# Attention's first loads and the projection's weights, issued during the stage before

## The chip, the cores and the metric

One program on one core of a Trainium2 chip. The time is the device time of one launch in microseconds (us); the median of three runs is compared. The engines have a queue each and run it in order: TensorE (PE, matrix products), VectorE (DVE), ScalarE (ACT), GpSimd (POOL) and SyncE (SP, which only issues transfers). A transfer (DMA) is issued by one of these engines and moves data between DRAM and the on-chip memory SBUF; those that POOL issues share one queue (q0, software_dynamic, in the profile), those of SP another (q1, hardware_dynamic). TensorE adds its products up in PSUM banks.

## The reference

One decoder layer over 2048 tokens of width 1024 in float32. The part that the change touches is the first of three sub-layers: one input projection, forgetting attention (8 heads of 64) beside a gated linear attention (4 heads), and one output projection.

```python
def forgetting_attention(q, k, v, f_logit):
    ...
    c = jnp.cumsum(log_f, axis=-1)
    ...
        s = jnp.einsum('bhqd,bhkd->bhqk', q[:, :, q0:q1], k[:, :, :q1], preferred_element_type=jnp.float32) * scale
        s = s + c[:, :, q0:q1, None] - c[:, :, None, :q1]
        ...
        p = jax.nn.softmax(jnp.where(causal, s, -jnp.inf), axis=-1)
        outs.append(jnp.einsum('bhqk,bhkd->bhqd', p.astype(v.dtype), v[:, :, :q1]))
    ...
def hybrid_mixer(...):
    fq, fk, fv, ff, gq, gk, gv, gg, ga = jnp.split(h @ w_in, offsets, axis=-1)
    fox = rms_norm(forgetting_attention(...), fox_out_gain)
    gla = rms_norm(gla_chunked(...), gla_out_gain) * jax.nn.silu(gg)
    return jnp.concatenate([fox, gla], axis=-1) @ w_out
```

Then follow cross-attention into 256 memory tokens (`w_xk`, `w_xv`, ...) and a mixture of 16 experts, whose routing needs small constant tables (index ramps, masks, ones).

## The kernel before

float32 operands are split into a high part (rounded to float32r) and a low part (the rest), and a product is three matmuls: high by high, low by high, high by low (`mm3`, L90 to L92). `split` makes the high part on ACT (L68, L71) and the low part on DVE (L69, L72).

**Stage 1** (to about 711 us) makes the projections. The columns of FoX's keys come last: 16 tiles of two heads by 512 tokens, token chunk by token chunk. Each is split into `o1` buffers and stored by SP (L170) to the DRAM scratch tensors `kh_d` and `kl_d`, [8 heads, rows, 2048]; the queries went to `qh_d` and `ql_d` before, the values to `fv_d`. The linear attention runs beside it on all engines; POOL's last operation for it is at L439.

**Stage 2** is the forgetting attention. Its 16 units are a head pair `p` (4) by a query chunk `c` of 512 (4). `load` (L492) fetches a unit's queries `q1`, `q2` and keys `k1`, `k2` of 256 to 272 KB each, unit 0's on POOL, the others on SP; the values `v` always on POOL, a quarter for each chunk of the first head pair, 1 MB at once for a later pair. Loads run two units ahead (AHEAD = 2). For each unit, `maxima` makes the scores a first time (`ps_a`, L526 and L527) and reduces them on DVE (L529, L531) to the rows' maxima; TensorE turns these round (`pmt`, L537), ACT and DVE split them (`mh`, `ml`), and POOL's queue writes them as two rows of 4 KB into `q2` (L541). `probs` then makes the scores again with the maxima subtracted inside the product (`ps_b`, L570 without and L571 with these two rows), takes the exponential on ACT (`pT`, L573), masks and sums on POOL and DVE, and multiplies by the values (`po`, L557). The unit's result `fe_o` is scaled (L612 to L621) and stored to `yT_d` by SP (L622). A scheduler hangs steps of the later units' maxima (`side`) between the steps of a unit's `probs`, so each engine's order is set when the program is built. `memory_in` prepares the 256 memory tokens in the last four units.

`route_init` (L1045 to L1079) makes the routing tables with some 9 small operations on POOL and as many on DVE. It is called last in stage 2, but depends on nothing in it, and the tables' memory is that of stage 1's last inputs, so that the scheduler has put it at the stage's start, ahead of POOL's first loads.

**Stage 3a** multiplies the joined outputs by `w_out`. Its eight row blocks are loaded by SP into the two buffers `wst` (L690) and split into `woh` and `wol`; a block's load waits for the split two before it. `enter` loads a tile of 128 tokens (`yT`, `y`, `x`; tile 0 on POOL, the rest on SP), and `mixed` makes two halves of 24 matmuls each into `ps`, adds them to `x` (L743) and stores `x` from POOL (L745). The memory tokens' keys and values (`ps_m`, L811, weights `mw` loaded by SP at L799 into two buffers) run beside it.

Of the kernel before, what the change touches and what calls it, by code (L numbers as in the profile page):

```python
# [25 lines left out]
def f32(ap):  # L26
    return ap.bitcast(F32)
# [26 lines left out]
class Trunk:  # L54
# [74 lines left out]
    def stage1(self):  # L129
# [3 lines left out]
        with tc.tile_pool(name="xT", bufs=1) as xp, tc.tile_pool(name="w1", bufs=2) as wp, \  # L133
# [25 lines left out]
            def ttype(ws, m, c, dst, parts=None, scale=1.0):  # L159

                ps = pp.tile([128, 512], F32, name="ps_mm", bufs=3)
                for k in range(KT):
                    self.mm3(ps, ws[k][:, 0, m * 128:(m + 1) * 128], ws[k][:, 1, m * 128:(m + 1) * 128],
                             xh[c][:, k], xl[c][:, k], k == 0, k == KT - 1)
                if parts:
                    hi, lo = (op[0].tile([128, 512], F32R, tag="o1", name="o1", bufs=3) for _ in range(2))
                    self.split(hi, lo, ps, scale)
                    for h in range(2):
                        for t, o in zip(parts, (hi, lo)):
                            nc.sync.dma_start(t[dst + h, 0:64, c * 512:(c + 1) * 512], f32(o)[h * 64:h * 64 + 64])  # L170
                    return
                o = op[0].tile([128, 512], F32, name="o1", bufs=n_o[0])
                evac(o, ps)
                nc.sync.dma_start(dst, o)
# [14 lines left out]
            with tc.tile_pool(name="o1a", bufs=2) as op[0], tc.tile_pool(name="xin", bufs=2) as ip, tc.tile_pool(name="psx1", bufs=2, space=PSUM) as px:  # L189
# [29 lines left out]
                def narrow(c):  # L219
                    cs = slice(c * 512, (c + 1) * 512)  # L220
                    ps = pp.tile([48, 512], F32, name="ps_mm", bufs=3)
                    for k in range(KT):
                        self.mm3(ps, wnh[:, k], wnl[:, k], xh[c][:, k], xl[c][:, k], k == 0, k == KT - 1)
                    o = op[0].tile([48, 512], F32, tag="o1", name="o1", bufs=n_o[0])
                    evac(o, ps)

                    t8, m8 = ip.tile([8, 512], F32, name="t8", bufs=1), ip.tile([8, 512], F32, name="m8", bufs=1)
                    c8 = ip.tile([8, 512], F32, name="c8", bufs=2)
                    nc.scalar.activation(t8, o[0:8], AF.Abs, bias=bf)
                    nc.vector.tensor_scalar(m8, o[0:8], bf, 0.0, op0=OP.add, op1=OP.min)  # L230
                    nc.scalar.activation(t8, t8, AF.Exp, scale=-1.0)
                    nc.scalar.activation(t8, t8, AF.Ln, bias=1.0)
                    nc.vector.tensor_tensor(m8, m8, t8, OP.subtract)
                    nc.vector.tensor_tensor_scan(c8, one8, m8, self.c_last[:, 511:512] if c else 0.0, OP.mult, OP.add)
                    self.c_last = c8
                    ch, cl = (ip.tile([8, 512], F32R, tag=tag, name=nm, bufs=1) for tag, nm in (("t8", "ch"), ("m8", "cl")))
                    self.split(ch, cl, c8, -1.0)
                    for r, t in ((64, ch), (65, cl)):
                        nc.sync.dma_start(self.kl_d[:, r, cs], f32(t))
                    nc.sync.dma_start(self.ga_d[:, cs], o[32:48])  # L240

                pin = self.tc.keep_in_program_order
# [6 lines left out]
                for c in range(4):  # L249
                    cs = slice(c * 512, (c + 1) * 512)  # L250
                    tn = turn(c + 1) if c < 3 else iter(())
                    for m in range(2):
                        for n in range(2):
# [3 lines left out]
                            if (c, m, n) == (0, 0, 0):  # L257
# [12 lines left out]

                                for t, r in ((self.qh_d, 64), (self.qh_d, 65), (self.kl_d, 66), (self.kl_d, 67)):
                                    for b in range(4):
                                        nc.gpsimd.dma_start(t[:, r, b * 512:(b + 1) * 512], one8)
                                w3 = w_in.rearrange("(t p) n -> p t n", p=128)
                                pin(nc.sync.dma_start(wn[:, :, 0:8], w3[:, :, FF:FF + 8]))
                                pin(nc.sync.dma_start(wn[:, :, 32:48], w3[:, :, GA:GA + 16]))
# [197 lines left out]
    def stage2(self):  # L474
# [3 lines left out]
        with tc.tile_pool(name="fx", bufs=1, reuse_waits="tile") as fp, \  # L478
# [13 lines left out]
            def load(u):  # L492

                p, c = u["p"], u["c"]
                cs = slice(c * 512, (c + 1) * 512)
                issue = nc.sync.dma_start if p or c else nc.gpsimd.dma_start
                dma = lambda out, src: issue(f32(out), src.rearrange("h d s -> d h s"))
                hs = slice(2 * p, 2 * p + 2)
                k1, k2 = K[p, c] = [big[f"{nm}{c}{p % 2 if c < 3 else 0}"]() for nm in ("k1", "k2")]
                q1, q2 = u["q"] = [big[f"{nm}{c}"]() for nm in ("q1", "q2")]  # L500
                dma(q1[0:64], self.qh_d[hs, 0:64, cs])
                dma(q1[64:128], self.ql_d[hs, :, cs])
                for d in (0, 64):
                    dma(k1[d:d + 64], self.kh_d[hs, :, cs])
                dma(q2[0:66], self.qh_d[hs, :, cs])
                dma(k2[0:68], self.kl_d[hs, :, cs])
                if c == 0:
                    V[p] = big[f"v{p % 2}"]()
                if c == 0 or p == 0:
# [33 lines left out]
            def probs(u):  # L543
# [73 lines left out]
                nc.gpsimd.tensor_tensor(w, r, r, OP.mult)  # L617
                yield
                nc.vector.scalar_tensor_tensor(w, w, -0.5, l2, op0=OP.mult, op1=OP.mult)
                nc.gpsimd.tensor_tensor(o, o, r, OP.mult)  # L620
                nc.vector.scalar_tensor_tensor(o, w, 1.5, o, op0=OP.add, op1=OP.mult)  # L621
                nc.sync.dma_start(self.yT_d[p * 128:p * 128 + 128, c * 512:(c + 1) * 512], o)  # L622

            ms = [fp.tile([128, 128], F32, name=f"m{i}", bufs=1) for i in range(2)]
            for m in ms:
                nc.gpsimd.memset(m, 0.0)
# [10 lines left out]
            mem = self.memory_in(fp, pp)  # L637
            def ahead():

                for u in units[:AHEAD]:  # L640
                    load(u)
                for n, u in enumerate(units):
                    if n + AHEAD < len(units):
                        load(units[n + AHEAD])
                    yield from maxima(u)
                    u["ready"] = True

            side, tail, due = ahead(), iter(()), 2.0
            for n, u in enumerate(units):

# [16 lines left out]
                pass  # L667
            for _ in mem:
                pass
            self.route_init(self.rp)  # L670


    def load_w(self, pool, hi, lo, src, gain, width, tag="wst"):
# [8 lines left out]
    def stage3a(self):  # L682
        tc, a = self.tc, self.a
        with tc.tile_pool(name="wo", bufs=1, reuse_waits="tile") as wp, tc.tile_pool(name="p3a", bufs=2, reuse_waits="tile") as ip, \
                tc.tile_pool(name="ps3a", bufs=2, space=PSUM, reuse_waits="tile") as pp:
            mem = self.memory_out(pp)
            wh, wl = [], []
            for k in range(KT):
                st = wp.tile([128, D], F32, name="wst", bufs=2)
                self.loaded = self.nc.sync.dma_start(st, a["w_out"].rearrange("l k n -> (l k) n")[k * 128:(k + 1) * 128])  # L690
                for ws, nm in ((wh, "h"), (wl, "l")):
                    ws.append(wp.tile([128, D], F32R, name=f"wo{nm}{k}"))
                self.split(wh[k], wl[k], st, self.gcol("fox_out_gain", k) if k < 4 else self.gcol("gla_out_gain", k - 4))
                if k % 4 == 3:
                    next(mem)
# [99 lines left out]
    def memory_weights(self, n):  # L795

        w = self.memory_block().rearrange("p (t n) -> p t n", t=KT)
        hs = slice(n % 4 * 128, n % 4 * 128 + 128)
        self.nc.sync.dma_start(w, self.a[("w_xk", "w_xv")[n // 4]].rearrange("l (t p) n -> p (l t) n", p=128)[:, :, hs])  # L799
        return w  # L800

    def memory_out(self, pp):
# [790 lines left out]
    def run(self, stages=("1", "2", "m", "3a", "3b", "4")):  # L1593
        with self.tc.tile_pool(name="const", bufs=1) as self.cpool, \
# [1 line left out]


            for nm, rows in (("qh_d", 66), ("ql_d", 64), ("kh_d", 64), ("kl_d", 68)):
                setattr(self, nm, self.dpool.tile([8, rows, S], F32, name=nm))
            self.consts()  # L1600
            for nm, shape in (("fv_d", [S, 512]), ("gqk_d", [2, 2, 128, S]), ("gv_d", [S, 512]),
                              ("gg_d", [S, 512]), ("ga_d", [16, S]), ("y_d", [S, 512]), ("yT_d", [512, S]), ("h1_d", [S, D]), ("h2_d", [S, D])):
# [43 lines left out]
```

## Time and profile before

| | us |
|---|---|
| median of three runs | 2461.46 (2458.09 to 2462.5) |
| the profiled execution | 2460.61 |
| its span on the profile | 2458.8 |
| TensorE busy in the span | 2325.2 (95%) |
| DVE, ACT, POOL busy | 1431.4 (58%), 955.4 (39%), 655.9 (27%) |
| mean granted TensorE clock | 0.973 of full |

TensorE works for 95% of the span, so what is left are the places in which it stands still or runs at a lower granted clock. The profile's list of 40 slices shows where: two slices in which TensorE is busy for less than 6 tenths, one between stages 1 and 2 (from about 711 us) and one between stages 2 and 3a (from about 1204 us). A granted clock of 1.00 is 2.4 GHz, 0.50 is 1.2 GHz; a stretch between the two holds some of both. "Waits" name the instruction that an engine stood before and the one that released it; a landing time is from a transfer's issue to its arrival.

### The profile page before, as it was taken

Reading aid. Unit: us, or ns where it says so; the run is one execution under the profiler, and the core shown is the slowest. Engines: PE = TensorE matmul, PEld = TensorE weight load, DVE = VectorE, ACT = ScalarE, POOL = GpSimd, SP = SyncE. Lnnn points to the kernel's source line nnn. Section 1 sums busy time; section 2 is a strip of 40 time slices with the busy share of each in tenths; the row PEclk is TensorE's granted clock in tenths of the full one; section 3 lists DMA queues with packets and bytes.
Section 4 is the critical chain, followed back from the end, with each engine's and each line's share of the span. In section 5 each row is a group of like instructions: output and inputs, shape, how many; then the busy total and the mean of one; then the engine's idle time right before and its main releaser. Section 6 shows DMA issues by size and latency. Waiting matters only on the chain. (4 is left out here: it accounts for less than half of the span.)

```text
span 2458.8 us, 39269 instructions
## 1 busy us (share of the span) xinstructions
PE 2325.2 (95%) x14569; PEld 1875.8 (76%) x14569; DVE 1431.4 (58%) x3561; ACT 955.4 (39%) x2058; POOL 655.9 (27%) x758
## 2 busy tenths in 40 slices
PE   7999999999978999999799999999599999999997
PEld 5778887777756656565478888888499989889996
DVE  5430035656526878778442236556567868768775
ACT  5321023434312444444431135544354545444543
POOL 2000012122213566676500000111322233324132
PEclk9999999999987999999999999999799999999998
DMA  5222122445465132311174521111478888879784
GB/s 180 72 93 69 69 83 83 135 114 133 103 161 131 49 92 59 82 35 53 62 241 126 146 109 53 52 53 53 141 238 260 247 271 257 247 250 270 259 237 133
DMA packets 287626, 337.81 MB, mean 137 GB/s; under 512 B 33264, under 2 KB 208938, under 8 KB 287429
## 3 DMA queue, kind: packets, MB, share of 16 engines
q1 hardware_dynamic: 258485, 257.26, 35.2%
q0 software_dynamic: 28944, 77.98, 10.8%
q8 instruction: 116, 1.90, 0.3%
q14 instruction: 81, 0.66, 0.1%
HBM read 252.27 MB, written 93.02 MB: 140 GB/s over the span
## 5 line engine op out<-in xcount | busy, mean ns | idle before, releaser
L90 PE MATMUL gu<-xTh,wer 128*128 128x288 f32 x1024 | 303.3, 301 | 0.5 <-ACT xTh L68 0.5
L91 PE MATMUL gu<-xTl,wer 128*128 128x288 f32 x1024 | 302.8, 297 | 0.0
L92 PE MATMUL gu<-xTh,wer 128*128 128x288 f32 x1024 | 301.9, 296 | 0.0
L69 DVE TENSOR_TENSOR wer<-wes,wer 128x1024 fp32r<-128x1024 f32 x192 | 232.1, 1220 | 37.4 <-ACT wer L68 37.2
L68 ACT ACTIVATE wer<-wes 128x1024 fp32r<-128x1024 f32 x192 | 198.0, 1052 | 112.2 <-PE yd L92 48.1
L573 ACT ACTIVATE pT<-ps_b 128x512 f32<-128x512 f32 (+3 forms) x320 | 159.7, 532 | 172.5 <-PE ps_b L571 169.1
L90 PEld LDWEIGHTS gu<-xTh,wer 128*128 128x128 f32 x1024 | 192.0, 189 | 3.8 <-ACT xTh L68 0.9
L91 PEld LDWEIGHTS gu<-xTl,wer 128*128 128x128 f32 x1024 | 192.9, 188 | 2.0 <-DVE xTl L69 0.6
L92 PEld LDWEIGHTS gu<-xTh,wer 128*128 128x128 f32 x1024 | 192.9, 188 | 1.8
L592 POOL TENSOR_TENSOR l<-l,pT 128x512 f32<-128x512 f32 (+3 forms) x128 | 151.7, 1185 | 55.1 <-ACT pT L573 48.7
L529 DVE TENSOR_REDUCE mm<-ps_a 128x1 f32<-128x512 f32 x192 | 128.0, 682 | 44.5 <-PE ps_a L527 43.5
L90 PE MATMUL ps_mm<-xh,w1r 128*128 128x512 f32 x384 | 153.3, 402 | 0.5 <-ACT xh L68 0.5
L91 PE MATMUL ps_mm<-xl,w1r 128*128 128x512 f32 x384 | 153.1, 399 | 0.0
L92 PE MATMUL ps_mm<-xh,w1r 128*128 128x512 f32 x384 | 152.4, 399 | 0.0
L91 PE MATMUL ps_mm<-w1r,xh 128*128 128x512 f32 x384 | 150.1, 393 | 0.0
L92 PE MATMUL ps_mm<-w1r,xl 128*128 128x512 f32 x384 | 149.8, 392 | 0.0
L90 PE MATMUL ps_mm<-w1r,xh 128*128 128x512 f32 x384 | 148.3, 392 | 0.0
L526 PE MATMUL ps_a<-k,q 128*128 128x512 f32 (+2 forms) x320 | 129.4, 407 | 16.2 <-DMA k<-kh_d 12.2
L557 PE MATMUL po<-pT,v 128*64 128x512 f32 (+3 forms) x640 | 132.2, 556 | 5.7 <-POOL pT L576 5.4
L527 PE MATMUL ps_a<-k,q 66*128 66x512 f32 (+2 forms) x320 | 124.8, 394 | 13.4 <-DMA k<-kl_d 13.4
L570 PE MATMUL ps_b<-q,k 128*128 128x512 f32 (+3 forms) x320 | 126.3, 403 | 4.0 <-ACT pT L573 4.0
L592 DVE TENSOR_TENSOR l<-l,pT 128x512 f32<-128x512 f32 (+3 forms) x128 | 109.0, 852 | 21.1 <-ACT pT L573 12.5
(429 smaller groups left out, 5599.7 us busy)
## 6 DMA issues: line engine op xcount, KB each, us to landing
wes<-in_w_expert_down_dram SPq DMA_DIRECT2D x64, 512.0 KB
wes<-in_w_expert_gate_dram SPq DMA_DIRECT2D x62, 512.0 KB
wes<-in_w_expert_up_dram SPq DMA_DIRECT2D x62, 512.0 KB
yr_d<-ye SPq DMA_DIRECT2D x32, 512.0 KB
w1s<-in_w_in_dram SPq DMA_DIRECT2D x48, 256.0 KB
xt<-in_x_dram SPq DMA_DIRECT2D x16, 512.0 KB
h_d<-x POOLq DMA_DIRECT2D x16, 512.0 KB, 3.5
h<-h_d SPq DMA_DIRECT2D x16, 512.0 KB
```

Of the source, the lines that this page charges most:

```text
L68: nc.scalar.activation(hi, src, AF.Copy)
L69: nc.vector.tensor_tensor(lo, src, f32(hi), OP.subtract)
L90: mm(ps, ah, bh, start=start, stop=False)
L91: mm(ps, ah, bl, start=False, stop=False)
L92: mm(ps, al, bh, start=False, stop=stop)
L526: nc.tensor.matmul(ps[:, :w], q1[:, i, qs], k1[:, i, :w], start=True, stop=False)
L527: nc.tensor.matmul(ps[:, :w], q2[0:66, i, qs], k2[0:66, i, :w], start=False, stop=True)
L529: nc.vector.tensor_reduce(mm[:, i, b, j:j + 1], ps[:, :w], AX.X, OP.max)
L557: ins = nc.tensor.matmul(po[i * 64:i * 64 + 64, off:], V[p][:, kb, i * 64:i * 64 + 64], pts[i][:, off:], start=new and o == 0, stop=len(to ...
L570: nc.tensor.matmul(ps[:, off:], k1[:, i, ks], q1[:, i, off:], start=True, stop=False)
L573: nc.scalar.activation(pt[:, off:], ps[:, off:], AF.Exp)
L592: add(sums[i][:, off:], sums[i][:, off:], pt[:, off:], OP.add)
```

## The change

Four things are altered.

1. The scratch tensors `qh_d`, `ql_d`, `kh_d`, `kl_d` become four tensors each, one for a chunk of 512 tokens, so that a load of chunk 0 depends on the stores of chunk 0 alone.
2. The loads of units 0 to 2 are written ahead of everything else in stage 2 and go to POOL (unit 3 and all later ones to SP); `route_init` is held until the last unit's last two operations are issued.
3. `yT_d` is stored from ACT instead of SP.
4. `w_out` is loaded into four buffers, two of them the `x3` tiles of the token loop; the split weights of blocks 4 to 7 lie in a pool of their own. From the third on, the memory weights `mw` are loaded by POOL instead of SP.

```diff
-                            nc.sync.dma_start(t[dst + h, 0:64, c * 512:(c + 1) * 512], f32(o)[h * 64:h * 64 + 64])
+                            nc.sync.dma_start(t[c][dst + h, 0:64], f32(o)[h * 64:h * 64 + 64])
...
-                cs = slice(c * 512, (c + 1) * 512)
-                issue = nc.sync.dma_start if p or c else nc.gpsimd.dma_start
+                issue = nc.sync.dma_start if p or c == 3 else nc.gpsimd.dma_start
...
-                dma(q1[0:64], self.qh_d[hs, 0:64, cs])
+                dma(q1[0:64], self.qh_d[c][hs, 0:64])
...
-                nc.gpsimd.tensor_tensor(o, o, r, OP.mult)
-                nc.vector.scalar_tensor_tensor(o, w, 1.5, o, op0=OP.add, op1=OP.mult)
-                nc.sync.dma_start(self.yT_d[p * 128:p * 128 + 128, c * 512:(c + 1) * 512], o)
-
+                last[:] = nc.gpsimd.tensor_tensor(o, o, r, OP.mult), nc.vector.scalar_tensor_tensor(o, w, 1.5, o, op0=OP.add, op1=OP.mult)
+                nc.scalar.dma_start(self.yT_d[p * 128:p * 128 + 128, c * 512:(c + 1) * 512], o)
+
+            for u in units[:AHEAD + 1]:
+                load(u)
...
-                for u in units[:AHEAD]:
-                    load(u)
                 for n, u in enumerate(units):
-                    if n + AHEAD < len(units):
+                    if n and n + AHEAD < len(units):
...
-            self.route_init(self.rp)
+
+            with tc.issue_after(last[0].ins), tc.issue_after(last[1].ins):
+                self.route_init(self.rp)
...
-                st = wp.tile([128, D], F32, name="wst", bufs=2)
+                st = (wp if k % 4 < 2 else ip).tile([128, D], F32, tag=("wst", "x3")[k % 4 // 2], name="wst", bufs=2)
...
-                    ws.append(wp.tile([128, D], F32R, name=f"wo{nm}{k}"))
+                    ws.append((wp, wp2)[k // 4].tile([128, D], F32R, name=f"wo{nm}{k}"))
...
-        self.nc.sync.dma_start(w, self.a[("w_xk", "w_xv")[n // 4]].rearrange("l (t p) n -> p (l t) n", p=128)[:, :, hs])
+        (self.nc.sync if n < 2 else self.nc.gpsimd).dma_start(w, self.a[("w_xk", "w_xv")[n // 4]].rearrange("l (t p) n -> p (l t) n", p=128)[:, :, hs])
...
-                setattr(self, nm, self.dpool.tile([8, rows, S], F32, name=nm))
+                setattr(self, nm, [self.dpool.tile([8, rows, 512], F32, name=f"{nm}{c}") for c in range(4)])
```

POOL's queue at the start of stage 2, before (the two rows at the top are stage 2's constants; routing tables stand ahead of them; `x4` are the four quarters of the first pair's values, and the 16-block `v` is the second pair's 1 MB):

```order
134 L633 MEMSET ones_6661 128x64
135 L634 MEMSET mean_6662 128x128
136 L497 DMA q_6672<-qh_d 64x2x512
137 L497 DMA q_6672<-ql_d 64x2x512
138 L497 DMA k_6670<-kh_d 64x2x512 x2
139 L497 DMA q_6673<-qh_d 66x2x512
140 L497 DMA k_6671<-kl_d 68x2x512
141 L512 DMA v_6680<-fv_d 128x4x128 x4
142 L512 DMA v_6910<-fv_d 128x16x128
143 L636 MEMSET mean_6662 64x64 x2
144 L541 DMA q_6673<-mh 1x8x128
145 L541 DMA q_6673<-ml 1x8x128
```

After, the same queue from the last of unit 2's loads on; the loads of units 0, 1 and 2, six of them and a quarter of `v` for each unit, stand ahead of this piece, right behind stage 1's last operation at L439:

```order
151 L496 DMA k_6692<-kl_d_74 68x2x512
152 L511 DMA v_6678<-fv_d 128x4x128
153 L626 MEMSET m_6702 128x128
154 L626 MEMSET m_6703 128x128
155 L631 MEMSET causal 128x384
156 L633 MEMSET ones_6707 128x64
157 L634 MEMSET mean_6708 128x128
158 L511 DMA v_6678<-fv_d 128x4x128
159 L511 DMA v_6922<-fv_d 128x16x128
160 L636 MEMSET mean_6708 64x64 x2
161 L540 DMA q_6671<-mh 1x8x128
162 L540 DMA q_6671<-ml 1x8x128
```

The routing tables are gone from here, the loads have moved ahead of the constants, and 18 loads of queries and keys instead of six stand on this queue ahead of the second pair's 1 MB and the two rows of maxima.

TensorE's queue around the first `ps_b` that needs unit 0's maxima, before (a step is one L526 and one L527; the `pmt` in this piece is unit 1's, unit 0's stands at row 2791):

```order
2826 L537 MATMUL pmt<-ident,m_6657 128x128
2827 L526 MATMUL ps_a<-k_6682,q_6695 128x512
2828 L527 MATMUL ps_a<-k_6683,q_6696 128x512
2829 L526 MATMUL ps_a<-k_6693,q_6695 128x256
2830 L527 MATMUL ps_a<-k_6694,q_6696 128x256
2831 L571 MATMUL ps_b<-q_6673,k_6671 128x512 x2
```

After, the same product, now at L570 (unit 0's `pmt` stands at row 2791 here too):

```order
2798 L525 MATMUL ps_a<-k_6668,q_6682 128x512
2799 L526 MATMUL ps_a<-k_6669,q_6683 128x512
2800 L525 MATMUL ps_a<-k_6680,q_6682 128x512
2801 L526 MATMUL ps_a<-k_6681,q_6683 128x512
2802 L525 MATMUL ps_a<-k_6668,q_6682 128x512
2803 L526 MATMUL ps_a<-k_6669,q_6683 128x512
2804 L570 MATMUL ps_b<-q_6671,k_6669 128x512 x2
2805 L570 MATMUL ps_b<-q_6671,k_6669 128x384
```

Between unit 0's `pmt` and the first product that needs its maxima stand 6 steps instead of 19.

## Rows read from the trace of the kernel before

**Rows 1.** Windows: stretch, length, busy (count) by engine, PE clock, DMA share, GB/s.

```profile
711.50:723.50 12.00, 0.00 (x0) 0.00 (x0) 3.93 (x19) 2.15 (x5) 10.21 (x25) 0.61 0.94 274
723.50:726.00 2.50, 2.26 (x6) 1.58 (x6) 0.00 (x0) 0.00 (x0) 0.39 (x3) 0.50 1.08 196
...
731.70:737.60 5.90, 5.76 (x16) 4.46 (x16) 4.24 (x18) 0.00 (x0) 0.00 (x0) 0.50 1.05 244
...
745.10:771.90 26.80, 26.77 (x76) 22.12 (x77) 18.47 (x46) 5.00 (x12) 7.74 (x18) 0.50 0.64 149
```

**Rows 2.** Waits of PE, 711 to 776: total, times, longest.

```profile
PE ps_a L527 <- DMA k<-kl_d: 13.4, 2, 7.6
PE ps_a L526 <- DMA k<-kh_d: 12.2, 1, 12.2
```

**Rows 3.** Timeline of POOL, 679 to 776: start, duration, operation, idle before, releaser.

```profile
678.81 0.46 POOL L439 TENSOR_TENSOR X<-X,qk 128x128 f32<-128x128 f32 x1 [5.59 <-ACT X L437]
711.57 0.25 POOL L1045 IOTA rev<- 128x32 f32 x1 [32.30 <-PE ps_mm L92]
...
713.42 0.70 POOL L497 DMA_DIRECT2D q<-qh_d  x1
...
722.43 1.16 POOL L512 DMA_DIRECT2D v<-fv_d  x1 [1.05 <-DMA q<-qh_d]
```

**Rows 4.** Transfers, 711 to 745.4: sum, queue shares, landing of the 1 MB load.

```profile
DMA packets 3408, 8.03 MB, mean 234 GB/s; under 512 B 645, under 2 KB 645, under 8 KB 3408
...
q0 software_dynamic: 1312, 3.70, 45.1%
...
v<-fv_d POOLq DMA_DIRECT2D x1, 1024.0 KB, 23.0
```

**Rows 5.** Transfers, 679 to 711: the hardware queue's packets, MB, share.

```profile
q1 hardware_dynamic: 2702, 3.15, 41.1%
```

**Rows 6.** Timeline of DVE, 709 to 776: stage 1's last split, two maxima steps.

```profile
712.15 0.69 DVE L72 SCALAR_TENSOR_TENSOR o<-ps_mm,o 128x512 fp32r<-128x512 f32 x1
...
732.23 0.29 DVE L531 CUSTOM_DVE_ANT_0 jk<-ps_a,causal 128x128 bf16<-128x128 f32 x1 [11.21 <-PE ps_a L527]
...
737.24 0.08 DVE L531 DVE_READ_ACCUMULATOR2_ANT mm<- 128x1 f32 x1
```

**Rows 7.** Transfers, 740 to 1100: landing of the maxima's 4 KB rows.

```profile
q<-ml POOLq DMA_DIRECT2D x14, 4.0 KB, 2.3
```

**Rows 8.** Waits of PE on ACT, 776 to 1203.

```profile
PE ps_b L570 <- ACT pT L573: 4.0, 2, 2.3
```

**Rows 9.** The store of `yT_d` by line: issue ns min/median/max, first and last.

```profile
L622 SPq DMA_DIRECT2D yT_d<-fe_o x16: 319/346/349, 790.2 to 1217.6; - x16
```

**Rows 10.** Waits of PE, 1203 to 1262.

```profile
PE ps L90 <- ACT yh L68: 9.6, 1, 9.6
PE ps L90 <- ACT woh L71: 3.6, 3, 1.8
...
PE ps L91 <- DVE wol L72: 1.2, 2, 0.6
```

**Rows 11.** Windows at the start of stage 3a.

```profile
1218.70:1228.30 9.60, 0.02 (x2) 0.01 (x1) 2.26 (x3) 3.20 (x4) 0.00 (x0) 0.71 0.87 294
1228.30:1235.00 6.70, 6.70 (x20) 5.50 (x21) 2.77 (x4) 2.30 (x2) 0.00 (x0) 0.65 0.52 157
1235.00:1255.30 20.30, 15.49 (x60) 11.18 (x59) 9.33 (x11) 7.34 (x9) 0.00 (x0) 0.92 0.69 234
```

**Rows 12.** Timelines of ACT and of POOL at the start of stage 3a.

```profile
1225.24 1.15 ACT L71 ACTIVATE woh<-wst,vcols 128x1024 fp32r<-128x1024 f32 x1 [6.11 <-DMA wst<-in_w_out_dram]
...
1227.63 0.61 ACT L68 ACTIVATE yh<-yT 128x512 fp32r<-128x512 f32 x1
...
1216.14 0.85 POOL L717 DMA_DIRECT2D yT<-yT_d  x1
```

**Rows 13.** Transfers, 1217 to 1255: landing of tile 0's `y`.

```profile
y<-y_d POOLq DMA_DIRECT2D x1, 256.0 KB, 5.4
```

More of the change, by code (lines that the diff above doesn't have):

```diff
@@ L238, in narrow @@
                     for r, t in ((64, ch), (65, cl)):
-                        nc.sync.dma_start(self.kl_d[:, r, cs], f32(t))
+                        nc.sync.dma_start(self.kl_d[c][:, r], f32(t))
                     nc.sync.dma_start(self.ga_d[:, cs], o[32:48])
@@ L272, in stage1 @@
                                     for b in range(4):
-                                        nc.gpsimd.dma_start(t[:, r, b * 512:(b + 1) * 512], one8)
+                                        nc.gpsimd.dma_start(t[b][:, r], one8)
                                 w3 = w_in.rearrange("(t p) n -> p t n", p=128)
@@ L500, in load @@
                 q1, q2 = u["q"] = [big[f"{nm}{c}"]() for nm in ("q1", "q2")]
-                dma(q1[0:64], self.qh_d[hs, 0:64, cs])
-                dma(q1[64:128], self.ql_d[hs, :, cs])
+                dma(q1[0:64], self.qh_d[c][hs, 0:64])
+                dma(q1[64:128], self.ql_d[c][hs])
                 for d in (0, 64):
-                    dma(k1[d:d + 64], self.kh_d[hs, :, cs])
-                dma(q2[0:66], self.qh_d[hs, :, cs])
-                dma(k2[0:68], self.kl_d[hs, :, cs])
+                    dma(k1[d:d + 64], self.kh_d[c][hs])
+                dma(q2[0:66], self.qh_d[c][hs])
+                dma(k2[0:68], self.kl_d[c][hs])
                 if c == 0:
@@ L646, in ahead @@
                     u["ready"] = True
+            last = []
             side, tail, due = ahead(), iter(()), 2.0
@@ L684, in stage3a @@
         with tc.tile_pool(name="wo", bufs=1, reuse_waits="tile") as wp, tc.tile_pool(name="p3a", bufs=2, reuse_waits="tile") as ip, \
+                tc.tile_pool(name="wo2", bufs=1, reuse_waits="tile") as wp2, \
                 tc.tile_pool(name="ps3a", bufs=2, space=PSUM, reuse_waits="tile") as pp:
```

## The prediction

> **What bounds the kernel now.** TensorE is busy for 95% of the span, so only the places where it stands still or runs slowly are worth anything. The list of 40 slices names two, and I took windows, waits and timelines of each.
>
> *Between stages 1 and 2* the windows show TensorE idle for 12 us, then two short bursts, then busy without a gap from 745.1 to 771.9 but at a granted clock of 0.50, that is 1.2 GHz [rows 1]. Its waits there are all for keys, 25.6 us in three pieces [rows 2]. POOL's timeline says why: idle from its last linear-attention operation at 678.8, it stood 32.30 us before the first routing table until the last matmul of stage 1 had released that table's memory, and issued unit 0's first load only at 713.4 [rows 3]. From then on the transfers ran full: 8.03 MB in 34.4 us, of which POOL's queue got 3.70 MB [rows 4]. In the 32 us before, the transfers' share was 41%, 3.15 MB [rows 5].
>
> Up to 771.9 TensorE did 2.26 + 5.76 + 26.77 = 34.8 us of work at half clock, 17.4 us at full clock. That is the mark that I compare: when does the new kernel have these 17.4 us done? After it, TensorE is busy in either kernel.
>
> *Between stages 2 and 3a* TensorE waits 9.6 us for the first tile's `yh` and 4.8 us more for `woh` and `wol` [rows 10], with the clock at 0.65 and 0.92 behind it [rows 11]. `yh` lay in ACT's queue behind two `woh` splits, which had waited for `w_out` [rows 12].
>
> **The change, part by part.**
>
> *Unit 0's data.* Units 0 to 2 are 18 loads and three quarters of `v`, 5.6 MB, queued on POOL from 678.8 with nothing in front. The stores of the keys they read stand ahead of that point in SP's queue, so no store still to come holds them. Unit 0's 1.86 MB take 16 us at the rate that POOL's queue had beside a busy SP, 3.70 MB in 32 us = 116 GB/s [rows 4], and are in SBUF by about 695. The 25.6 us of waits go. What is late next is DVE's last split of stage 1, which ends at 712.8 [rows 6] and frees the PSUM bank: TensorE starts at 713 instead of 723.6. Unit 0's eight maxima took DVE 732.23 to 737.3, 0.64 us each [rows 6], and this pace holds TensorE too. By the order it has 17 steps ahead of the first product that needs unit 0's maxima (8 of unit 0, 3 of unit 1 ahead of `pmt`, 6 behind it), which is 713 + 17 x 0.64 = 724.
>
> *Unit 0's maxima (the step I am least sure of).* At 724 TensorE comes to the first `ps_b` that needs the two 4 KB rows; behind `pmt` stand 6 steps instead of 19. POOL can issue these rows at about 720, but on its queue the last quarter of `v` and the second pair's 1 MB now lie just in front. That 1 MB waits for stage 1's last key stores, as it did before, and landed 23.0 us after its issue [rows 4]. When is it through? The queue has 5.6 + 0.26 + 1.05 = 6.9 MB to move. At the total rate of 234 GB/s [rows 4] the 32.5 us before 711.5 hold 7.6 MB, less 3.15 MB of stage 1 [rows 5] leaves 4.4 MB; the other 2.5 MB at 116 GB/s take 21.5 us: 733. With 116 GB/s throughout it is 738; with the 1 MB served alone from its issue at about 719 it is 728. I take 733, and 735 for the rows behind it. No row here has a 4 KB write issued behind an unfinished megabyte, so both ends stay: 2.3 us after issue [rows 7] would be 723, and 3 us more than the slowest of these sums 741.
> The Trainium skill, "DMA: Bandwidth & Descriptors", section "Two DMAs through the same engine are not ordered", says that within one queue of one DMA engine descriptors start in order though they may finish out of it. By that rule the two rows cannot start before the megabyte has started, which is the 735; without it they would land by 723, the first rival below. No run here shows which.
>
> So TensorE stands for about 11 us again, 724 to 735. Before, 12 us without work brought the clock to 0.50, and it stayed there for 26.8 us of unbroken work [rows 1]. In stage 3a, after a gap of 9.6 us, the stretch with the lower clock was about 7 us [rows 11]. I take the nearer, stage 2. The 17 steps are some 6.9 us of work at full clock: before, they took the 2.26 and 5.76 us of rows 1 and about 5.8 of the 26.77, halved. 10.5 of the 17.4 are left, 21 us at half clock: 756, against 771.9. **Gain 16 us**. Bounds: rows by 728 and the clock back after 7 us give 728 + 7 + 7 = 742, 30 us; rows at 741 and half clock throughout give 762, 10 us.
>
> *Routing tables.* Some 20 small operations leave the start, where DVE's and POOL's lay in waits anyway, and come back at the end of stage 2, where TensorE has 7 us of `ps_m` to do. There they cost what they put ahead of tile 0's load on POOL, with the 512 KB `mw` load that is now POOL's too: issue at about 1217.7 instead of 1216.14 [rows 12].
>
> *Stage 3a.* The first four blocks of `w_out` are in SBUF before stage 2 ends, so the splits no longer hold `yh`. It follows its load: 1217.7 + 5.4 (tile 0's `y` on the same queue [rows 13]) + 0.6 for the split = 1223.7, against 1228.3: 4.6 us. Blocks 4 to 7 are asked for as the first four are split and land at about 1233, near the time TensorE wants them, so most of the 4.8 us of waits for `woh` and `wol` [rows 10] goes; I take 4. The clock I leave as it is. **Gain 8.6 us**. Bounds: 12.6 with all of the waits gone and the 6.7 us at 0.65 run at full clock (3.3 us); 3 if tile 0's `x`, which now comes after a split of block 6 or 7 and two `mw` loads on POOL, holds the sums back.
>
> *`yT_d` from ACT.* 16 issues of 0.35 us [rows 9] in ACT's queue, and ACT stands in each until DVE has finished `fe_o`. I laid the new places of the stores beside the old trace: ACT would stand up to 5 us there, but in stretches in which it had no `ps_b` to take anyway. TensorE waited 4.0 us for ACT in all of 776 to 1203 [rows 8]. Cost 0, at most 4 us. The per-chunk scratch tensors cost nothing: same bytes, same number of transfers.
>
> Sum: 2460.6 - 16 - 8.6 = 2436 for an execution like the profiled one; the median of the runs shown is 0.85 us above that execution: **2437 us**. Its own range goes from 30 + 12.6 gained (2419) to 10 + 3 gained less 4 (2452).
>
> **The rivals.**
>
> *The maxima are not held* (chance 0.22). The two rows land 2 to 3 us after issue, as 14 later pairs did [rows 7]. TensorE goes on at 724 at a clock that has not fallen; 10.5 us more make 735 against 771.9: 37 us, with 8.6 from stage 3a 2416. For it: the 41% transfer share [rows 5], which may let units 0 to 2 and part of the rest through early. Against it: the 1 MB cannot be issued before stage 1's last stores are in.
>
> *The early loads don't come early* (0.12). Something that I have not seen holds POOL's first load until stage 1 has ended; unit 0 then comes through the same crowded queues, and only stage 3a gains: 2452 (2449 to 2458). For it: POOL's 32.30 us wait [rows 3] was of that kind, a memory dependence that the code doesn't show. Against it: in the new order nothing on POOL stands between its last L439 and the loads.
>
> *Stage 1's end is held up* (slower, 0.08). Its 16 key tiles go from `o1` buffers to DRAM over SP's queue while POOL's 5.6 MB now share the DMA engines. If those stores fall behind, the splits stop for lack of buffers, then PSUM, then TensorE. Stage 1 moves 3.15 MB in these 32.5 us; it takes under 3.15 MB in 62 us = 51 GB/s to lose the 30 us that would make the kernel 5 us slower in spite of the 25 gained: 2466 and more. Against it: in 711 to 745.4, with both queues full, all but POOL's 3.70 of 8.03 MB [rows 4], 126 GB/s, went to the others. The Trainium skill, same page, section "Queues, rings and completion order", says that each DMA engine takes turns between the queues, a packet at a time; by it the stores would keep their share, and the rival falls.
>
> **How the numbers follow.** Forecast 0.52, fast maxima 0.22, loads not early 0.12, stage 1 held up 0.08; 0.06 is left for gains that another stage gives back, most of it within 0.2% (5 us, about what a measurement of this kernel can tell from no change). The range 2414 to 2454 holds nearly all of the first, most of the second and about half of the third, 0.8. Faster by over 0.2%: 0.85; same: 0.06; slower: 0.09.
>
> **What would show it.** In the new profile POOL's first L496 issue should stand at about 679 and TensorE's first `ps_a` at about 713, with no wait for `k`. The disputed step shows as a wait of `ps_b` L570 for `q` written by `mh` or `ml`: 11 us at about 724 with a clock of 0.50 behind it is the forecast, under 3 us the first rival. If `kh_d` stores land later and TensorE waits before 711, it is the slower one. In stage 3a the wait for `yh` should be about 5 us. The forecast is wrong if TensorE recovers its clock at once (gain up to 30) or if tile 0's sums wait for `x`.

## The result, and the profile after

The changed kernel takes **2439.73 us** (median of five runs, 2431.71 to 2444.25) against 2461.15 us before (five runs), a ratio of 0.9913 with an interval of 0.9892 to 0.9934: 21.4 us faster (16 to 27). Forecast were 2437 us. The time came out as forecast; the two gains behind it did not: the first was smaller than forecast and the second larger.

Where the time went is best read from the end of each attention unit's products (ACT's start of `fe_o<-po`, one row of the timeline for a unit), in the traces of both kernels:

| unit | 0 | 1 | 2 | 3 | 7 | 11 | 15 | 3a's first product | 3a's last add |
|---|---|---|---|---|---|---|---|---|---|
| before, us | 776.55 | 796.82 | 830.70 | 878.48 | 992.85 | 1106.18 | 1208.83 | 1228.29 | 1441.60 |
| after, us | 758.65 | 784.32 | 820.20 | 867.13 | 981.24 | 1094.50 | 1196.83 | 1212.26 | 1417.63 |
| earlier by | 17.9 | 12.5 | 10.5 | 11.4 | 11.6 | 11.7 | 12.0 | 16.0 | 24.0 |

The last column is DVE's last addition of `ps` to `x`:

```profile
1441.60 0.69 DVE L743 TENSOR_TENSOR x<-ps,x 128x512 f32<-128x512 f32 x1 [4.75 <-PE ps L92]
1417.63 0.69 DVE L745 TENSOR_TENSOR x<-ps,x 128x512 f32<-128x512 f32 x1 [4.75 <-PE ps L92]
```

So 12 us come from the start of stage 2 and stay (unit 0's larger lead is steps of later units' maxima that stood ahead of its first `ps_b` and now come behind it), and 12 us from the start of stage 3a: 4.0 up to its first product, 8.0 more up to its first add (1254.27 before, 1230.21 after). From there to the last add both kernels take 187 us.

By these marks the gain is 24 us; the profiled span is 18.5 us shorter and the median 21.4. Behind 3a the program is the same, but one profiled execution differs there from another by several us: from 3a's last add to the first expert product 334.9 to 340.5 us in the traces of this study, from there to the end 681.0 to 692.8 (682.1 before, 687.8 after). Stage 2 varies too: from unit 3 to unit 15 it takes 324.5 to 334.5 us in the traces whose programs differ little there. So a gain is read from marks next to the place of the change, and 2 or 3 us at stage 2's end or in the total tell nothing.

The start of stage 2 in windows, the columns as in [rows 1]:

```profile
711.50:722.90 11.40, 1.88 (x10) 1.23 (x8) 1.44 (x3) 1.19 (x2) 0.16 (x1) 0.80 0.64 174
722.90:752.30 29.40, 19.38 (x57) 15.94 (x58) 13.97 (x45) 4.23 (x11) 5.78 (x13) 0.56 0.85 204
752.30:776.00 23.70, 23.63 (x109) 14.67 (x107) 19.45 (x42) 8.39 (x18) 12.96 (x17) 1.00 0.23 59
```

and TensorE's waits there (711 to 776), which answer to [rows 2]:

```profile
PE ps_a L525 <- DVE o L72: 9.5, 1, 9.5
PE ps_a L525 <- DVE mm L530: 5.9, 1, 5.9
PE ps_b L570 <- DMA q<-ml: 4.1, 1, 4.1
```

No wait for keys is left; three others have come, 19.5 us together against 25.6. The work in the stretch with the lower clock fell from 34.8 us to 19.4. That is 6.1 us of waits and, taking both stretches at half clock, (34.8 - 19.4) / 2 = 7.7 us of clock, less 1.9 us by which stage 1's last matmul came later in this trace (712.99 against 711.10): 11.9 us, the 12 of the table.

POOL's timeline answers to [rows 3]: the first load stands at 680.8, right behind the last linear-attention operation, and the megabyte of `v` waits from 711 to 729.8.

```profile
680.80 0.68 POOL L496 DMA_DIRECT2D q<-qh_d  x1
...
710.90 0.76 POOL L511 DMA_DIRECT2D v<-fv_d  x1
729.82 1.16 POOL L511 DMA_DIRECT2D v<-fv_d  x1 [18.16 <-DMA q<-qh_d]
...
738.75 0.56 POOL L540 DMA_DIRECT2D q<-mh  x1 [7.42 <-ACT mh L71]
739.30 0.54 POOL L540 DMA_DIRECT2D q<-ml  x1
```

What TensorE waits for at 722.9 is stage 1's last split. DVE's and ACT's timelines show these splits waiting for `o1` buffers, that is for the stores of earlier key tiles (the first line names a store of `y`, which goes over the same queue):

```profile
708.50 0.69 DVE L72 SCALAR_TENSOR_TENSOR o<-ps_mm,o 128x512 fp32r<-128x512 f32 x1 [7.25 <-DMA y_d<-y]
719.53 0.69 DVE L72 SCALAR_TENSOR_TENSOR o<-ps_mm,o 128x512 fp32r<-128x512 f32 x1 [10.34 <-DMA kh_d<-o]
...
717.46 0.60 ACT L71 ACTIVATE o<-ps_mm 128x512 fp32r<-128x512 f32 x1 [12.34 <-DMA kl_d<-o]
```

Before, the same splits waited for TensorE alone. The transfers of 679 to 711, which answer to [rows 5], say why (queue: packets, MB, share):

```profile
q0 software_dynamic: 2043, 4.90, 66.1%
q1 hardware_dynamic: 2275, 2.24, 29.6%
```

SP's queue moved 2.24 MB in this stretch instead of 3.15, because POOL's moved 4.90 beside it. In packets the two are near each other; in bytes POOL has twice as much.

At the start of stage 3a (1196 to 1262) two waits are left, against [rows 10]:

```profile
PE ps L90 <- ACT yh L68: 5.6, 1, 5.6
PE pss L611 <- POOL fe_sq L600: 1.0, 1, 1.0
```

ACT's timeline there: two blocks of `w_out` are split at once, and `yh` waits for its own load only (against [rows 12]).

```profile
1206.94 2.17 ACT L71 ACTIVATE woh<-wst,vcols 128x1024 fp32r<-128x1024 f32 x2
1211.57 0.63 ACT L68 ACTIVATE yh<-yT 128x512 fp32r<-128x512 f32 x1 [2.46 <-DMA yT<-yT_d]
```

The wait for `yh` is 4.0 us shorter and the 4.8 us for `woh` and `wol` are gone. With them goes the second stretch at a lower clock: the windows that answer to the last two of [rows 11] are

```profile
1212.30:1219.00 6.70, 6.70 (x21) 5.55 (x22) 4.39 (x4) 3.13 (x3) 0.00 (x0) 0.68 0.92 299
1219.00:1230.20 11.20, 11.20 (x54) 9.22 (x53) 7.24 (x9) 6.62 (x10) 1.44 (x2) 1.00 1.02 344
```

0.68 as before (0.65), and then 1.00 instead of 0.92 and without a gap. That is worth some 1.8 us (6.7 x 0.35 and 20.3 x 0.08 before, 6.7 x 0.32 after); some 1.4 of the 12 us are left without an account.

### The profile page after: what moved, and what is told of

It reads as the page before. It is cut to its first block, busy times and chain, and to the rows that moved or that the text cites. A ratio compares the mean times of both kernels' runs of the same rounds, so it can differ in the third digit from the quotient of the medians.

```text
span 2440.3 us, 39272 instructions
## 1 busy us (share of the span) xinstructions
PE 2321.5 (95%) x14569; PEld 1873.1 (77%) x14569; DVE 1433.6 (59%) x3561; ACT 953.7 (39%) x2058; POOL 678.7 (28%) x776
## 5 line engine op out<-in xcount | busy, mean ns | idle before, releaser
L591 DVE TENSOR_TENSOR l<-l,pT 128x512 f32<-128x512 f32 (+3 forms) x128 | 111.7, 873 | 23.3 <-ACT pT L572 11.6
L570 PE MATMUL ps_b<-q,k 68*128 68x512 f32 (+3 forms) x320 | 116.8, 376 | 4.1 <-DMA q<-ml 4.1
```

The costliest lines, as they stand in the source:

```text
L570: nc.tensor.matmul(ps[:, off:], k2[0:68, i, ks], q2[0:68, i, off:], start=False, stop=True)
L591: add(sums[i][:, off:], sums[i][:, off:], pt[:, off:], OP.add)
```

## The experiments

Ratios are to the kernel before, run on the same chip beside them; the changed kernel's is 0.9913. "Stage 2's end" is the last unit's `fe_o`, 1196.83 in the changed kernel's trace.

### What the early start hangs on: the routing tables (rt_early)

```diff
-            with tc.issue_after(last[0].ins), tc.issue_after(last[1].ins):
-                self.route_init(self.rp)
+            self.route_init(self.rp)
```

> As the changed kernel, but the routing tables are not held back. By the order they then stand on POOL ahead of the 18 loads, as they stood ahead of unit 0's before. If they are what kept the loads from starting (they wait for memory that stage 1's last matmul frees): POOL's first load at about 713 instead of 681, TensorE's waits for k return, no wait for o any more, and with three units on one queue the start of stage 2 is no better than before: 2455 to 2468. If not, the loads start at 681 and the time is that of the changed kernel.

Measured: ratio 1.0047 (1.0028 to 1.0067), slower than before. POOL's timeline and TensorE's waits (711 to 776):

```profile
711.90 0.25 POOL L1046 IOTA rev<- 128x32 f32 x1 [32.30 <-PE ps_mm L92]
...
712.87 0.69 POOL L496 DMA_DIRECT2D q<-qh_d  x1
...
752.73 1.16 POOL L511 DMA_DIRECT2D v<-fv_d  x1 [0.68 <-DMA k<-kh_d]
757.28 0.56 POOL L540 DMA_DIRECT2D q<-mh  x1 [3.05 <-ACT mh L71]
```

```profile
PE ps_a L525 <- DVE mm L530: 17.5, 1, 17.5
PE ps_a L525 <- DMA k<-kh_d: 11.8, 1, 11.8
PE ps_b L570 <- DMA q<-ml: 9.6, 1, 9.6
PE ps_a L526 <- DMA k<-kl_d: 5.4, 1, 5.4
```

POOL stands before the first table until stage 1's last matmul, as in the kernel before; the loads start at 713, 32 us later, and TensorE waits 44 us. So the gain does not come without holding the tables back, and putting three units on POOL's one queue is by itself a loss: unit 0 ends at 786.29, 9.7 us later than before. The mechanism is the one that the prediction read from the 32.30 us wait [rows 3]. What holding the tables back alone would give to the kernel before, with unit 0 alone on POOL, was not run.

### The halves (loads_only, proj_only, proj_mw_sp)

`loads_only` is the changed kernel without its part for stage 3a (two `wst` buffers, `yT_d` and `mw` from SP); `proj_only` is the kernel before with that part.

```diff
-                st = (wp if k % 4 < 2 else ip).tile([128, D], F32, tag=("wst", "x3")[k % 4 // 2], name="wst", bufs=2)
+                st = wp.tile([128, D], F32, name="wst", bufs=2)
...
-                nc.scalar.dma_start(self.yT_d[p * 128:p * 128 + 128, c * 512:(c + 1) * 512], o)
+                nc.sync.dma_start(self.yT_d[p * 128:p * 128 + 128, c * 512:(c + 1) * 512], o)
...
-        (self.nc.sync if n < 2 else self.nc.gpsimd).dma_start(w, ...)
+        self.nc.sync.dma_start(w, ...)
```

> Only the first half of the change (chunked scratch, units 0 to 2 loaded early on POOL, routing tables late); the projection's weights, the store of yT_d and the memory weights are as before. Theory S (the early loads slow the stores of stage 1's last key tiles, and the three o1 buffers then hold the splits): the boundary looks as in the changed kernel, TensorE's first ps_a at about 723, waits of 9.5, 5.9 and 4.1 us there; 12 us gained in all, about 2449. If the two halves help or hinder each other, it is not 2449.

Measured: 0.9942 (0.9921 to 0.9963), 14 us faster (9 to 19), in agreement with 12. From unit 15's `fe_o` to 3a's last add its trace takes 232.0 us, as the kernel before (232.8); the changed kernel takes 220.8. TensorE's waits in the two places, 600 to 1300:

```profile
PE ps L90 <- ACT yh L68: 10.5, 1, 10.5
PE ps_a L525 <- DVE o L72: 7.8, 1, 7.8
```

> Only the second half (four buffers for w_out, yT_d stored from ACT, memory weights on POOL); the start of stage 2 is as before. If the halves add up: 6 us gained, about 2455, with TensorE's wait for yh near 5.6 us instead of 9.6 and the waits for woh and wol gone.

Measured: 0.9996 (0.9978 to 1.0014), no gain that can be told from none (5 us at most), where 6 us were expected (the 18.5 us of the span less 12). The trace says otherwise: unit 15's `fe_o` stands at 1208.91 as before, and 3a's last add at 1434.13 is 7.5 us earlier. Trace and totals disagree here. In the two profiled executions the part behind the first expert product takes most of the 7.5 us back (687.5 us here, 682.1 before); whether that is chance or belongs to the change stays open. In 3a the waits for `woh` and `wol` are gone, but `yh` is waited for longer than in the changed kernel:

```profile
PE ps L90 <- ACT yh L68: 8.7, 1, 8.7
```

POOL's timeline shows what stands ahead of tile 0's `yT` there: two loads of `mw`, where the changed kernel has one (the second comes behind `y`).

```profile
1216.68 0.97 POOL L800 DMA_DIRECT2D mw<-in_w_xk_dram  x1
1219.55 0.90 POOL L800 DMA_DIRECT2D mw<-in_w_xk_dram  x1 [1.89 <-PE ps_m L812]
1220.43 0.76 POOL L718 DMA_DIRECT2D yT<-yT_d  x1
```

`proj_mw_sp` takes them off POOL (the last lines of the diff above, in `proj_only`):

> The second half alone, with the memory weights on SP as before. In the second half alone two mw loads of 512 KB stood ahead of tile 0's yT on POOL, and TensorE waited 8.7 us for yh. If that is why that half gained nothing: yT is issued about 3 us earlier, the wait falls to 5 or 6, and 3 us are gained on it (about 0.2%); if the queue makes no difference, the wait stays.

Measured: 0.9975 (0.9957 to 0.9994), with this wait:

```profile
PE ps L90 <- ACT yh L68: 6.7, 1, 6.7
```

2.0 us less, somewhat short of the 3 expected; from unit 15's `fe_o` to 3a's last add it takes 221.4 us against `proj_only`'s 225.2, near the changed kernel's 220.8. By the ratios the total is 5 us better than `proj_only`'s, with intervals that overlap. `mw` on POOL is therefore a weak point of this half by itself. In the whole change it does no harm, as the same edit there shows:

> As the changed kernel, but the memory weights mw are all loaded by SP again. If their loads on POOL stand before tile 0's yT there and slow it, TensorE's wait for yh falls from 5.6 us to about 4; if SP, which waits for the w_out blocks, is the worse place, the third memory product waits instead. Total within 3 us of the changed kernel.

Measured: 0.9939 (0.9918 to 0.9959). The wait did not fall; it lies within the 5.5 to 7.9 us of the other traces that have both halves and late tables:

```profile
PE ps L90 <- ACT yh L68: 6.6, 1, 6.6
```

### What holds stage 1's end: stores or the new scratch layout (one_unit, more_o1)

`one_unit` loads only unit 0 early; units 1 and 2 go to SP as before.

```diff
-                issue = nc.sync.dma_start if p or c == 3 else nc.gpsimd.dma_start
+                issue = nc.sync.dma_start if p or c else nc.gpsimd.dma_start
...
-            for u in units[:AHEAD + 1]:
-                load(u)
+            load(units[0])
```

> As the changed kernel, but only unit 0 is loaded early on POOL (and the first pair's values); units 1 and 2 are loaded by SP behind stage 1's stores, as before. Theory S: far fewer bytes beside the stores, so DVE's splits are not held, and TensorE's first ps_a stands at about 714 to 716 instead of 722.9. Rival R (the chunked scratch tensors or the new memory layout make the stores slow by themselves): first ps_a stays at about 722. In either case units 1 and 2 come later, so that TensorE may wait for their keys (k<-kh_d) at about 722 to 735: the total 2435 to 2450.

Measured: 0.9926 (0.9902 to 0.9949). TensorE's first `ps_a` stands at 714.98. Its waits (711 to 776), and the transfers of 679 to 711.5:

```profile
PE ps_a L526 <- DMA k<-kl_d: 9.4, 2, 7.9
PE ps_a L525 <- DVE mm L530: 7.2, 1, 7.2
PE ps_a L525 <- DVE o L72: 1.4, 1, 1.4
```

```profile
q1 hardware_dynamic: 3082, 3.20, 40.6%
q0 software_dynamic: 1040, 2.65, 33.6%
```

With 2.65 MB instead of 4.90 beside them SP's transfers are back at 3.20 MB and the wait for the split is 1.4 us, though the scratch tensors are the new ones. Theory S stands; rival R falls. But unit 1's keys are then late, and unit 1 ends at 786.15 against 784.32: what is not moved before 711 is missing afterwards. Whether the early loads need the scratch tensors in four pieces was not run: no version keeps the undivided ones.

`more_o1` gives the splits a fourth buffer (`bufs=4`, two are used by a tile; more do not fit beside the linear attention's tiles).

> As the changed kernel, with four o1 buffers instead of three (no more fit). Theory S: a split finds a free buffer earlier, so TensorE's wait for o at the end of stage 1 falls from 9.5 us to about 4 to 6 and the total by 3 to 5, about 2435. Rival R2 (the wait is not for buffers but for the DMA engines' total rate): the wait stays at 9 us.

Measured: 0.9907 (0.9879 to 0.9936), the changed kernel's time. The wait:

```profile
PE ps_a L525 <- DVE o L72: 8.2, 1, 8.2
```

1.3 us less, not 4: a miss. Even the 1.3 us cannot be put down to the buffers, since the same wait is 7.1 to 9.5 us in the traces with three (`mem_later` 7.1, `best` 7.3, `loads_only` 7.8, `mw_sp` 8.1, `v1_sp` 8.4). One buffer more does not lift the stall; fewer bytes beside the stores do (1.4 us in `one_unit`).

### The two other waits (mem_later, v1_sp)

The wait of 5.9 us for DVE's `mm` is DVE standing in its queue before `rs_v` of the memory tokens, which waits for ACT's squares (L783) and they for a load that SP issues behind stage 1's late stores:

```profile
727.84 1.06 ACT L783 ACTIVATE sq<-mw 128x1024 bf16<-128x1024 f32 x1 [5.73 <-DMA mw<-in_mem_dram]
729.02 0.15 DVE L81 TENSOR_SCALAR rs_v<-mss 128x1 f32<-128x1 f32 x1 [6.05 <-ACT sq L783]
```

`mem_later` holds these steps until the last units:

```diff
                     if n >= 12:
-                        next(mem, None)
+                        with tc.issue_after(last[1].ins), tc.issue_after(act[0].ins), tc.issue_after(hold[0].ins):
+                            next(mem, None)
```

> As the changed kernel, but the first steps of the memory tokens (two 512 KB loads on SP, the squares on ACT, four small operations and one of 1.28 us on DVE) are held until a late unit of stage 2. Theory M (TensorE's 5.9 us wait for DVE's mm L530 at the start of stage 2 is DVE standing in its queue before rs_v, behind ACT's squares and the memory load): this wait falls to under 1 us, and the first unit's maxima are there some 6 us sooner; 3 to 7 us less in all, about 2434, unless the rows of maxima then wait as much longer behind the second pair's 1 MB. Rival: the wait is DVE's own pace, and stays.

Measured: 0.9933 (0.9907 to 0.996). TensorE's waits (711 to 776):

```profile
PE ps_a L529 <- DVE o L72: 7.1, 1, 7.1
PE ps_b L574 <- DMA q<-ml: 5.1, 1, 5.1
PE ps_a L529 <- DVE mm L532: 0.4, 1, 0.4
```

The wait is gone, unit 3 ends at 863.37, 3.8 us before the changed kernel's, and unit 11 at 1087.63, 6.9 us before it (of which some 3 may be the scatter of stage 2). But units 12 to 15, where the steps now lie, give it back: stage 2 ends at 1204.19, 7.4 us later. The squares wait 5.6 us for their load there, ahead of the exponentials in ACT's queue, and the granted clock is 0.83 in 1100 to 1150, against 0.97 in the changed kernel. Theory M stands, and this place for the steps gives no gain.

`v1_sp` moves the second pair's megabyte of `v` to SP:

```diff
-                    nc.gpsimd.dma_start(V[p][:, b], ...)
+                    (nc.sync if p == 1 else nc.gpsimd).dma_start(V[p][:, b], ...)
```

> As the changed kernel, but the second pair's 1 MB of v goes to SP's queue, behind unit 3's loads and the second pair's first keys. Theory V (the two 4 KB rows of unit 0's maxima wait behind this megabyte on POOL's queue): TensorE's wait of 4.1 us for q<-ml at L570 goes, the rows land within 3 us of their issue; about 3 us less, 2437. Rival: the rows are slow because all transfers are, and land after 6 to 8 us as before.

Measured: 0.9933 (0.9907 to 0.9959). TensorE's wait for the rows:

```profile
PE ps_b L570 <- DMA q<-ml: 2.8, 1, 2.8
```

The rows now land 6.1 us after the second one's issue (737.62 to 743.75) instead of 7.3, with nothing large ahead of them on their queue. So the rival has the larger part. The megabyte adds about 1 us in this pair: `combo`, with the same edit, has 6.6 us, and the changed kernel, `more_o1`, `loads_only` and `mw_sp`, all with the megabyte in front, have 7.3 to 7.5. But `best` and `two_best`, without it, have 8.9 and 9.7. Nor are the rows slow only because all engines are full: in `v1_sp` the DMA share is over 1.1 until 740, but 0.27 from 741 to 744, with the rows still under way. What holds them there is not shown. Stage 2 ends at 1193.89, 2.9 us before the changed kernel's, less than such marks scatter; the totals can't tell the two apart.

### Putting them together (two_best, best, combo)

`two_best`: units 0 and 1 early, with `mem_later`, `v1_sp` and `mw_sp`.

> All remedies together: units 0 and 1 early on POOL, unit 2 on SP as before, the memory tokens' steps late, the second pair's v on SP, the memory weights on SP. By theory S, M and V: TensorE's first ps_a at 715 to 718 instead of 722.9, no wait for mm L530 and for q<-ml over 2 us, a shorter stretch at the lower clock: 8 to 15 us below the changed kernel, about 2428. If unit 2's keys are late instead, TensorE waits for k<-kh_d behind 730 and the gain over the changed kernel is under 5 us.

Measured: 0.9963 (0.9945 to 0.998), worse than the changed kernel. TensorE's timeline has its first `ps_a` where it was wanted, and unit 0 ends at 747.90, 10.8 us before the changed kernel's:

```profile
714.86 0.67 PE L529 MATMUL ps_a<-k,q 128*128 128x128 f32 x3 [1.41 <-DVE o L72]
```

It is all lost again by unit 3 (871.93 against 867.13): TensorE waits 4.8 us for the rows of unit 1's maxima and 2.8 us for DVE, each with a lower clock behind it (0.84 in 755 to 776, 0.81 in 835 to 850). Stage 2 ends at 1212.04, with the same loss in the last units as in `mem_later`.

`best` is `v1_sp` with the memory tokens' steps held until unit 3.

> As the changed kernel, with the two remedies that helped where they act: the memory tokens' first steps are held until unit 3 is done (not until the last units, where they cost what they had gained), and the second pair's 1 MB of v is on SP. If both gains last: unit 11's products end some 6 to 9 us before the changed kernel's, and so does stage 2; the total about 2432 on a chip where the changed kernel has 2440. If the transfers at the start of stage 2 are the limit whatever the order, the difference stays under 3 us.

Measured: 0.9971 (0.9955 to 0.9988): a miss. Units 1 and 2 end 2.7 us before the changed kernel's, unit 3 4.5 us after it. ACT's queue holds the squares there, and they wait 4.13 us for their load, which TensorE then waits for in turn (776 to 1200; in the changed kernel this line has 2.4 us):

```profile
PE ps_b L573 <- ACT pT L576: 6.3, 3, 4.1
```

```profile
841.08 1.06 ACT L790 ACTIVATE sq<-mw 128x1024 bf16<-128x1024 f32 x1 [4.13 <-DMA mw<-in_mem_dram]
```

Stage 2 ends at 1200.05, 3.2 us after the changed kernel's. So the memory tokens' steps cost 5.9 us in their old place and, by these marks, some 7 at unit 3 and 14 in the last units.

`combo` is `more_o1` with `v1_sp`.

> The changed kernel with four o1 buffers and the second pair's v on SP, the two edits after each of which stage 2 ended 2 to 3 us sooner in its trace. If they add: TensorE's waits for o and for q<-ml 7 to 8 and under 3 us, the last unit's products done at about 1191 to 1193 instead of 1196.8, and the median 4 to 6 us below the changed kernel. If the start is held by the bytes that have to move, one gives back what the other gains: end of stage 2 at 1194 to 1197.

Measured: 0.9922 (0.9901 to 0.9942). Waits, 600 to 1300:

```profile
PE ps_a L525 <- DVE o L72: 9.0, 1, 9.0
...
PE ps_b L570 <- DMA q<-ml: 4.8, 2, 3.6
```

Stage 2 ends at 1195.14, in the range of the second case. No version of this study is faster than the changed kernel by more than the runs can tell.

## Why the prediction was right, and where not

- **The two places.** Both were real, but they were not read rightly from the list of 40 slices, where both lie in slices at 7 tenths. The one slice below 6 tenths is the 29th, 1721 to 1783 us, ahead of the experts' products; the prediction does not speak of it, and it stands at 5 tenths after the change too.

```profile
PE   7999999999978999999799999999599999999997
```

- **What bounded the start of stage 2** (POOL held by the routing tables' memory): right: with the tables in front (`rt_early`) 1.0047 against 0.9913.
- **Unit 0's loads early, waits for keys gone**: right; first load at 680.8, no wait for `k` left.
- **"TensorE starts at 713"**: wrong, 722.9. This is the step that failed. It took DVE's last split from the trace of before, though that trace had no load beside it. The mechanism was in the prediction, as the slower rival, with a price of 30 us from 51 GB/s down; what was left out is that it has a smaller price above that rate. SP's queue kept 2.24 MB in 32 us, 70 GB/s, and the start came 10 us late. I had taken the 126 GB/s that SP's queue had in 711 to 745.4 [rows 4] as what it would get. The rule of the Trainium skill that was set beside this rival ("DMA: Bandwidth & Descriptors", section "Queues, rings and completion order": an engine takes turns between the queues, a packet at a time) fits the trace, if the profile's packets may be taken for the page's: 2275 on SP's queue against 2043 on POOL's. Read in bytes, as I did when I let the rival fall by it, it does not, since POOL's packets were 2.4 KB on average and SP's 1.0 KB. That the packets' size is the cause was not tried apart.
- **The pace of the maxima, 724 for the product that needs them**: DVE's pace for unit 0 was right (eight in 5.1 us from 731.47), but TensorE came to the product at 742.5, 19.6 us after its start instead of 10.9. The memory tokens' steps on DVE, which lay in a wait before, now stood in front: 5.9 us, not foreseen. The other 2.8 us go with a granted clock of 0.50 (722.9 to 738), where the forecast had full clock.
- **The rows of the maxima** ("11 us of waiting, landed at 735"): right in kind, mis-sized: 4.1 us of waiting, landed at 746.6. They were issued at 739.3 instead of about 720, and the megabyte at 729.8 instead of about 719. That the rows come behind the megabyte agrees with the trace of the changed kernel: the transfers' view has POOL's queue with 0.42 MB from 730 to 738.7, 0.64 MB from there to 746.5, the whole megabyte, and the rows land at 746.57. The section "Two DMAs through the same engine are not ordered" of the same page of the Trainium skill, by which they start behind it, agrees with this trace. But little hung on it: in `v1_sp`, without the megabyte in front, they came only some 1 us sooner after their issue.
- **The clock**: forecast was half clock for all that is left after the wait, 21 us of it, and before that 713 to 724 at full clock. Measured: 0.56 in the mean of 722.9 to 752.3, with 19.4 us of work, and full from there. After the last wait 5.7 us of unbroken work went by before the clock rose (746.57 to 752.3), nearer to stage 3a's 7 us before than to the 26.8 us that I took.
- **Gain of 16 us at the start of stage 2**: 12 measured. The start 10 us too late and the 5.9 us cost more than forecast, the shorter wait for the rows and the clock less: the errors went against each other, and the sum was nearer than its parts.
- **Gain of 8.6 us in stage 3a**: 12.0 by the marks (from unit 15's `fe_o` to the last add 232.8 before, 220.8 after), over the forecast and near its bound of 12.6. The wait for `yh` went from 9.6 to 5.6 us (4.6 forecast for the gain, 4.0 measured), those for `woh` and `wol` from 4.8 to nothing (4 forecast). The term that was set at nothing is the clock, which the prediction left as it was: some 1.8 us, since the second stretch at a lower clock went with the waits. (The bound has 3.3 us for the 6.7 us at 0.65; 6.7 x 0.35 are 2.3.) By the same marks this half gives 7.5 us alone and 11.3 with `mw` on SP; `proj_only`'s totals do not show it, and that stays open.
- **The sum**: the first gain came out 4 us under the forecast and the second 3.4 us over it. That the time lies so near to 2437 us is in part luck.
- **`yT_d` from ACT at no cost**: TensorE waited 2.4 us for `pT` in 776 to 1200, against 4.0 before [rows 8], so the waits show no cost. No run tries this store alone: from unit 3 to unit 15 the changed kernel takes 329.7 us, and with the store on SP `loads_only` takes 324.5 and the kernel before 330.4. A cost within the 4 us stated is neither shown nor excluded.

## What to carry to other kernels

A load that is moved into the stage before takes its bandwidth from that stage: before counting the start as free, price the stage's own stores at the rate that is left, and look at what their buffers hold up. When several waits lie on top of each other, the removal of the longest uncovers the next ones (here 9.5, 5.9 and 4.1 us of 25.6), and an operation that cost nothing in the old wait has a price in the new order. And look for what a whole queue stands behind: here a handful of table operations, waiting for memory, decided whether the change lost 12 us or gained 21. Last, read a gain from marks next to the place of the change: the total here varied by more than most of the steps were worth.

## What the runs showed that was not expected

- A transfer of 4 KB, 2.3 us from issue to landing as a rule [rows 7], took 6.1 us in `v1_sp`, 8.9 us in `best` (731.34 to 740.19) and 9.7 us in `two_best` (723.18 to 732.90), with nothing large ahead of it on its queue.
- The stores that ACT issues appear as a queue of their own, in the profile's list of queues of the changed kernel, 4.20 MB for 16 stores:

```profile
q10 hardware_dynamic: 2304, 4.20, 0.5%
```
